# Three seven-product K pairs at the start of the input projection's middle chunk pairs, in a two-layer hybrid trunk

## The chip, the cores and the metric

The kernel runs on one core of a Trainium2 chip, in one launch. The metric is device time in microseconds (us) of that core, as the median of several executions. The engines are named as the profile names them: PE is TensorE (PEld its weight loads), DVE is VectorE, ACT is ScalarE, POOL is GpSimd, SP is SyncE, whose queue carries the weights in. Tiles have 128 partitions.

## What is computed

Two layers over 256 tokens of width 2048, all in float32. Each layer has one combined input projection to 6144 columns, two attentions of eight heads, one output projection, and a gated feed-forward network (FFN):

```python
for l in range(DEPTH):
    h = rms_norm(x, pre_mix_norm[l])
    proj = h @ w_in[l]            # q, k, v of the stick-breaking heads, q, k, v of the differential heads
    m = concat(stick_breaking(proj), differential(proj)) @ w_o[l]
    x = x + rms_norm(m, post_mix_norm[l])
    h = rms_norm(x, pre_ffn_norm[l])
    f = (silu(h @ w_gate[l]) * (h @ w_up[l])) @ w_down[l]
    x = x + rms_norm(f, post_ffn_norm[l])
```

## The kernel before

**Products.** A float32 product is made of three matmuls on rounded operands: hi x hi, hi x lo and lo x hi, where hi is the operand rounded by ACT and lo the rest, taken by DVE (`product`, L1216 to L1221). "A product" below is such a triple of 128x128 by 128x512.

**Tiling.** Weights come in column chunks of 512 and in K pairs: 256 rows of the 2048, so eight K pairs, 0 to 7. One chunk of one K pair is one transfer of 512 KB on SP's queue (L253). The input projection takes its 12 chunks two by two: `PAIRS` lists six chunk pairs, n = 0 to 5. A chunk pair has four accumulators in PSUM, for two halves of the tokens (t = 0, 1) and two chunks: x11, x12 (t = 0), x21, x22 (t = 1). All pairs from n = 1 on use the same four banks.

**Eight or seven products.** A K pair of a chunk pair is a 2 x 2 by 2 x 2 block product. In the ordinary form it takes eight products, 24 matmuls (`eight_in`, L998). In the seven-product form (Strassen's scheme as Winograd arranged it) it takes seven, 21 matmuls, called p1, p6, p7, q5, c11, c12 and c21. They need sums of token blocks, made once per layer (`pair_forms`, L1008, `token_sums`, L1223), and sums of the weight blocks, made each time in place: `mixed_weights` (L276 to L318) takes both chunks of the K pair. The first, a, is rounded like any other (hi L330, lo L340). For the second, b, DVE adds one half (L308), ACT rounds and DVE takes the rest (hi L302, lo L304), DVE makes two more sums (L313, L314), and both are split again into Th and Tl (L302, L304), one of 512 columns and one of 1024. Th and Tl have one buffer each in this stage; hi and lo have six each, which is three K pairs.

**Where sevens were.** The middle pairs, n = 1 to 4, run their K pairs in the order 0, 1, 4, 2, 5, 3, 6, 7 (`IN_ORDER`), with K pairs 4 and 5 as sevens: `seven_products` puts p1, p6, p7 and q5 into four further banks, and `shared_part` (L1257 to L1264) combines these with one copy on ACT and four operations on DVE. When the pair is finished, `settle` adds the result to each accumulator (four additions on DVE, L1039). The last pair, n = 5, works differently: it starts with its two sevens, all in the four accumulators (`sevens_alone`, L1142). There ACT copies an accumulator aside at the moment when it holds exactly the shared part (`kept_part`, L1172), DVE subtracts these copies (L1187 to L1189), and `added_alone` (L1191) settles three accumulators. An ordinary K pair goes between the sevens' last products (`between`). The output projection starts in the same way, with K pairs 4 and 5 of chunks 0 and 1.

**Order.** Each engine works through its own list in program order. The attention of earlier chunk pairs is interleaved with the projection's matmuls. It is paced by a clock that counts TensorE's steps, and `burst` marks the times in which no attention may claim the banks that a seven needs. Weights are asked for through a plan made beforehand (`weight_order`). An ordinary chunk lands in the tag "raw" with four buffers, and the chunks of a seven in another room (`late_room`, tiles named GU). The output projection runs over K pairs in the order `KP_O` (L34). K pair k needs heads 2k and 2k+1 normalised (L715), transposed on TensorE (L729) and scaled into a `mix` tile.

## Time and profile before

| | us |
|---|---|
| median of three runs | 2179.39 |
| the three runs | 2178.74, 2184.57, 2179.39 |
| the profiled execution | 2180.22 |
| its span | 2178.5 |
| granted TensorE clock | 0.999 |
| middle pairs n = 2, 3, 4 of layer 0 | about 45 us each |

The profiled execution lies 0.83 us above the median. In rows of groups the columns are: line, engine, operation, output<-inputs, shapes, count, then busy time and mean ns of one, then idle time of the engine just before and what ended it. In rows of waits they are the time waited in all, how often, and the longest. In rows of a timeline they are start and duration. A row of transfers gives the count, the size and the median time from issue to landing.

### The profile page before, as it was taken

The numbers are of one execution on the slowest core, as the hardware profiler recorded it, in microseconds if no ns is written. First come the engines' busy times: TensorE is split into PE (matmuls) and PEld (weight loads), VectorE is DVE, ScalarE is ACT, GpSimd is POOL, SyncE is SP. The second block draws the span as 40 slices with busy tenths as digits, with TensorE's granted clock in tenths as the row PEclk, the third lists the DMA queues.
The fourth block names the chain that finished last, engine by engine and source line by source line (L and its number), as shares of the span: only waits on it lengthen the run. The fifth ranks groups of instructions, "written<-read, shape, count | busy, mean of one in ns | idle before, by whom it ended". The sixth has DMA issues, their size and how long they took to land.

```text
span 2178.5 us, 28781 instructions
## 1 busy us (share of the span) xinstructions
PE 2161.9 (99%) x9932; PEld 1778.3 (82%) x9932; DVE 1960.4 (90%) x2705; ACT 1414.4 (65%) x2113; POOL 246.5 (11%) x239
## 2 busy tenths in 40 slices
PE   9999999999999999999999999999999999999998
PEld 7888888888888888888878888888888888888886
DVE  7888977899999999999878888778999999999997
ACT  7666775765766666666665667757566666576664
POOL 2100000021221220000010000000212212200000
PEclk9999999999999999999999999999999999999999
DMA  8545446497887877767465564455978877767683
GB/s 324 194 165 200 161 171 199 156 307 230 248 260 225 232 234 233 224 228 253 146 242 174 179 206 155 171 179 184 294 232 253 257 224 237 232 218 241 203 269 99
DMA packets 140275, 470.44 MB, mean 216 GB/s; under 512 B 15952, under 2 KB 16976, under 8 KB 139616
## 3 DMA queue, kind: packets, MB, share of 16 engines
q1 hardware_dynamic: 121952, 436.03, 57.9%
q0 software_dynamic: 17600, 32.02, 8.9%
q8 instruction: 78, 1.28, 0.2%
q14 instruction: 69, 0.57, 0.1%
q10 hardware_dynamic: 576, 0.54, 0.1%
HBM read 460.14 MB, written 8.39 MB: 215 GB/s over the span
## 4 chain that ended last, share of the span: by engine, by line
PE 90%; DVE 5%; ACT 2%; DMA 2%; issue 2%; DVEq 0%; SPq 0%; ACTq 0%
PE c L1351 20%; PE in L1219 7%; PE in L1221 7%; PE in L1220 7%; PE dn L1582 4%; PE dn L1585 4%; PE dn L1583 4%; PE p L1220 3%; PE c L1219 2%; PE c L1220 2%; PE p L1221 2%; PE c L1221 2%; PE p L1219 2%; PE o L629 2%; PE o L631 2%; PE o L630 2%
## 5 line engine op out<-in xcount | busy, mean ns | idle before, releaser
L340 DVE TENSOR_TENSOR lo<-raw,hi 128x1024 fp32r<-128x1024 f32 x448 | 544.0, 1233 | 58.5 <-ACT hi L330 57.4
L330 ACT ACTIVATE hi<-raw 128x1024 fp32r<-128x1024 f32 x470 | 480.1, 1054 | 73.6 <-DMA raw<-in_weights_in_turn_dram 33.2
L1351 PE MATMUL c<-hi,xF 128*128 128x512 f32 x1344 | 364.4, 392 | 0.7 <-DVE xF L539 0.5
L1351 PEld LDWEIGHTS c<-hi,xF 128*128 128x128 f32 x1344 | 249.7, 188 | 53.3 <-ACT act L1469 1.9
L270 POOL DMA_DIRECT2D T<-in_weights_in_turn_dram x122 | 107.6, 882 | 1367.5 <-PE c L1351 541.0
L1351 PE MATMUL c<-lo,xF 128*128 128x512 f32 x672 | 207.4, 390 | 0.0
L302 ACT ACTIVATE Th<-T 128x512 fp32r<-128x512 f32 x122 | 77.2, 633 | 199.4 <-DVE T L313 198.4
L302 ACT ACTIVATE Th<-G 128x1024 fp32r<-128x1024 f32 x122 | 129.0, 1058 | 80.0 <-DVE G L314 78.6
L1582 PE MATMUL dn<-hi,jh 128*128 128x512 f32 x416 | 162.0, 389 | 0.0
L1583 PE MATMUL dn<-lo,jh 128*128 128x512 f32 x416 | 161.8, 389 | 0.0
L304 DVE TENSOR_TENSOR Tl<-G,Th 128x1024 fp32r<-128x1024 f32 x122 | 148.9, 1221 | 11.6 <-ACT Th L302 11.6
L304 DVE TENSOR_TENSOR lo<-T,hi 128x1024 fp32r<-128x1024 f32 x122 | 152.9, 1253 | 0.1
L330 ACT ACTIVATE hi<-G 128x1024 fp32r<-128x1024 f32 x122 | 128.9, 1056 | 36.5 <-DMA G<-in_weights_in_turn_dram 22.1
L314 DVE TENSOR_TENSOR G<-G,T 128x1024 f32<-128x1024 f32 x122 | 148.7, 1219 | 2.6 <-DVE T L313 0.9
L1351 PEld LDWEIGHTS c<-lo,xF 128*128 128x128 f32 x672 | 126.0, 188 | 26.4
L340 DVE TENSOR_TENSOR lo<-G,hi 128x1024 fp32r<-128x1024 f32 x104 | 126.8, 1219 | 10.1 <-ACT hi L330 9.9
L302 ACT ACTIVATE hi<-T 128x1024 fp32r<-128x1024 f32 x122 | 128.0, 1050 | 11.4 <-PE c L1221 8.3
L1585 PE MATMUL dn<-hi,jl 128*128 128x512 f32 x416 | 128.1, 389 | 0.0
L1219 PE MATMUL in<-hi,xT 128*128 128x512 f32 x316 | 125.9, 400 | 1.6 <-DVE xT L929 1.6
L1219 PE MATMUL in<-hi,xI 128*128 128x512 f32 x316 | 126.1, 400 | 0.0
L1220 PE MATMUL in<-lo,xI 128*128 128x512 f32 x316 | 123.5, 391 | 0.3 <-DVE lo L340 0.3
L1221 PE MATMUL in<-hi,xI 128*128 128x512 f32 x316 | 123.2, 391 | 0.0
(522 smaller groups left out, 5028.8 us busy)
## 6 DMA issues: line engine op xcount, KB each, us to landing
raw<-in_weights_in_turn_dram SPq DMA_DIRECT2D x482, 512.0 KB, 4.9
T<-in_weights_in_turn_dram SPq DMA_DIRECT2D x122, 512.0 KB, 5.3
G<-in_weights_in_turn_dram SPq DMA_DIRECT2D x122, 512.0 KB, 5.4
T<-in_weights_in_turn_dram POOLq DMA_DIRECT2D x122, 256.0 KB, 5.6
GU<-in_weights_in_turn_dram SPq DMA_DIRECT2D x48, 512.0 KB, 6.4
V<-in_weights_in_turn_dram SPq DMA_DIRECT2D x8, 512.0 KB, 5.3
away_ffn<-x SPq DMA_DIRECT2D x8, 512.0 KB, 7.2
xd<-away_ffn SPq DMA_DIRECT2D x8, 512.0 KB, 9.2
```

The lines of the kernel that those rows point to most:

```text
L302: nc.scalar.activation(h, w, AF.Copy)
L304: newest_rest[i] = nc.vector.tensor_tensor(out=l, in0=w, in1=h.bitcast(F32), op=ALU.subtract)
L314: nc.vector.tensor_tensor(out=g, in0=g, in1=t2.unsqueeze(1).to_broadcast([P, 2, CW]), op=ALU.add)
L330: nc.scalar.activation(hi, raw, AF.Copy)
L340: rest = nc.vector.tensor_tensor(out=lo, in0=raw, in1=hi.bitcast(F32), op=ALU.subtract)
L1219: nc.tensor.matmul(a, sh, hi, start=first, stop=False, skip_group_check=open_sums[0])
L1220: nc.tensor.matmul(a, sh, lo, start=False, stop=False, skip_group_check=open_sums[0])
L1221: return nc.tensor.matmul(a, sl, hi, start=False, stop=last, skip_group_check=open_sums[0])
L1351: nc.tensor.matmul(a, stat[part], w[j][:, kk, :], start=first and kk + n == 0, stop=last and kk == 1 and n == 2)
L1582: nc.tensor.matmul(accs[c, t], sh, hi[:, kk, :], start=first, stop=False, skip_group_check=open_sums[0])
L1583: nc.tensor.matmul(accs[c, t], sh, lo[:, kk, :], start=False, stop=False, skip_group_check=open_sums[0])
L1585: nc.tensor.matmul(accs[c, t], sl, hi[:, kk, :], start=False, stop=last, skip_group_check=open_sums[0])
```

## The change

The middle pairs now begin with three sevens, K pairs 4, 5 and 6, which share the four accumulators as those of the last pair did. `sevens_alone` takes two or three K pairs. With three, the product c21 of all of them has a bank of its own ("c21_in", `lone`), ACT keeps copies of all four accumulators, and DVE makes four operations (three subtractions, and one that reads the lone bank); `added_alone` then settles three accumulators. The ordinary K pair 0 stands in `between`. The rest follows in the order 1, 2, 3, 7. `seven_in` is gone. The weights of K pair 6 land in the "raw" ring of four buffers, its token sums in a tile of tag "v". In `KP_O`, K pairs 1 and 2 trade places. The last pair keeps its two sevens, and the FFN stays as it was.

```diff
-KP_O = (4, 5, 6, 7, 0, 1, 2, 3)
+KP_O = (4, 5, 6, 7, 0, 2, 1, 3)
...
-IN_SEVEN = (4, 5)
-IN_ORDER = (0, 1, 4, 2, 5, 3, 6, 7)
-IN_LAST = (4, 5, 0, 1, 2, 3, 6, 7)
-IN_NOW = ((), IN_SEVEN, IN_SEVEN, IN_SEVEN, IN_SEVEN, IN_SEVEN)
+IN_SEVEN = (4, 5, 6)
+IN_NOW = ((), IN_SEVEN, IN_SEVEN, IN_SEVEN, IN_SEVEN, IN_SEVEN[:2])
...
 def in_order(n):
 
-    if n == 0:
-        return tuple(range(KT // 2))
-    return IN_LAST if n == len(PAIRS) - 1 else IN_ORDER
+    return IN_NOW[n] + tuple(kp for kp in range(KT // 2) if kp not in IN_NOW[n])
...
                 if kp in IN_NOW[n]:
                     plain.add(lay["in"][cb, kp])
-        aside[lay["in"][PAIRS[-1][1], IN_LAST[1]]] = "v"
+                if kp in IN_NOW[n][2:]:
+                    in_ring.add(lay["in"][cb, kp])
+        aside[lay["in"][PAIRS[-1][1], IN_SEVEN[1]]] = "v"
         order_o = [(c, kp) for kp in KP_O for c in (0, 1)]
         order_o += [(c, kp) for kp in LATE_O for c in (2, 3)] + [(c, kp) for c in (2, 3) for kp in LAST_O]
...
-            elif i in plain or i + 1 in plain:
+            elif {i, i + 1} & (plain - in_ring):
                 raw = late_room([P, 2, CW], f"GU{i}")
             else:
                 raw = wpool.tile([P, 2, CW], F32, tag="raw", bufs=4, name=f"raw{i}")
-            mixing = bool({i, i + 1} & (own | plain))
+            mixing = bool({i, i + 1} & (own | plain - in_ring))
             with not_ahead(i) if mixing else nullcontext():
...
         def sums_of(kp):
-            forms[kp] = pair_forms(pool, pool.sums, len(IN_SEVEN), xT, kp, f"in{l}")
+            if kp == IN_SEVEN[2]:
+                forms[kp] = pair_forms(pool, pool, 2, xT, kp, f"in{l}", tags=("v",))
+            else:
+                forms[kp] = pair_forms(pool, pool.sums, 2, xT, kp, f"in{l}")
...
-                        if alone:
-                            if t + col:
-                                src = added_alone(src, w, t, col, w[(0, 0, 2, 3)[2 * t + col]])
-                        elif w is not None:
-                            src = w[:, 2 * t + col, :]
-                            nc.vector.tensor_tensor(out=src, in0=banks[2 * t + col], in1=src, op=ALU.add)
+                        if mine and t + col:
+                            src = added_alone(src, w, t, col, w[0 if t == 0 else 2 + col], len(mine) == 3)
                         st = heads.setdefault((kind // 3, g), {"w": {}, "pT": {}, "scored": 0})
...
-                extra = None
-                burst[0] = clock[0] + 4 * kps.index(mine[0]) if mine and not alone else None
-                if alone:
+                if mine:
                     open_sums[0] = True
-                    w = pool.tile([P, 4, CW], F32, tag="gpost", bufs=1, name=f"w{l}_{n}")
-                    at = [plan[l]["in"][c, kp] for kp in kps[:2] for c in cc]
+                    if not ending:
+                        burst[0] = clock[0]
+                        assert math.inf not in taken
+                    room = pool.tile([P, 4, CW], F32, tag="gpost", bufs=1, name=f"w{l}_{n}")
+                    w = [room[:, i, :] for i in range(4)]
+                    at = [plan[l]["in"][c, kp] for kp in mine for c in cc]
+                    ordinary = kps[len(mine)]
 
                     def between(t):
-                        eight_in(banks, xT, l, cc, kps[2], (t,), False, False, 2)
-
-                    w = [w[:, i, :] for i in range(4)]
-                    sevens_alone(banks, forms, xT, kps[:2], at, w, between)
-                    kps = kps[3:]
+                        eight_in(banks, xT, l, cc, ordinary, (t,), False, False, 2)
+
+                    sevens_alone(banks, forms, xT, mine, at, w, between, f"c21_in{l}_{n}")
+                    kps = kps[len(mine) + 1 :]
                     ahead = list(KP_O[:2])
+                    if not ending:
+                        burst[:] = (clock[0] + 4 * len(kps) if n + 2 < len(PAIRS) else None), clock[0] + SETTLE
...
-                    if kp in mine and not alone:
-                        if extra is None:
-                            assert math.inf not in taken
-                            extra = four_banks(True, [f"{q}_in{l}_{n}" for q in ("p1", "p6", "p7", "q5")])
-                        seven_in(banks, extra, forms[kp], xT, l, cc, kp, kp == mine[0], kp == mine[-1])
-                        if kp == mine[-1]:
-                            burst[:] = None, clock[0] + SETTLE
-                            w = pool.tile([P, 4, CW], F32, tag="gpost", bufs=1, name=f"w{l}_{n}")
-                            with tc.high_priority(offset=URGENT):
-                                shared_part(extra, [w[:, i, :] for i in range(4)])
-                            if n + 2 < len(PAIRS):
-                                burst[0] = clock[0] + 4 * (len(kps) - 1 - j) + 4 * IN_ORDER.index(IN_NOW[n + 1][0])
-                        continue
...
-    def sevens_alone(banks, sums, tiles, kps, at, w, between):
+    def sevens_alone(banks, sums, tiles, kps, at, w, between, nm):
 
         x11, x12, x21, x22 = banks
-        feed(at[0] + 5)
-        jobs = []
-        for n, kp in enumerate(kps):
+        lone = bank(nm) if len(kps) == 3 else x21
+        feed(at[0] + (6 if len(kps) == 3 else 5))
+        def products_of(n):
+            kp = kps[n]
             hi, lo = ready[at[2 * n]]
             m = ready[at[2 * n + 1]]
             a11, a12, a22 = pair_blocks(tiles, kp)
             s1, s2, s3, s4 = sums[kp]
-            first = n == 0
-            jobs.append({
+            first, last = n == 0, lone is not x21 and n == len(kps) - 1
+            return {
                 "p1": (x11, a11, (hi[:, 0, :], lo[:, 0, :]), first, False),
                 "q5": (x12, s1, m["t1"], first, False),
                 "p7": (x21, s3, m["t3"], first, False),
                 "p6": (x22, s2, m["t2"], first, False),
                 "c11": (x11, a12, (hi[:, 1, :], lo[:, 1, :]), False, False),
                 "c12": (x12, s4, m["b22"], False, False),
-                "c21": (x21, a22, m["t4"], False, False),
-            })
-        a, b = jobs
+                "c21": (lone, a22, m["t4"], first and lone is not x21, last),
+            }
 
         def run(*todo):
             for n, job in enumerate(todo):
@@ -1171,34 +1159,49 @@
             with tc.high_priority(offset=URGENT):
                 nc.scalar.copy(w[j], bank)
 
-        run(a["p1"], a["q5"], a["p7"], a["p6"], b["p1"], b["q5"])
-        kept_part(0, x11)
-        kept_part(3, x12)
-        run(a["c11"], b["c11"])
-        feed(at[0] + 6)
-        run(b["p6"])
-        kept_part(1, x22)
-        run(a["c12"], b["c12"], b["p7"])
-        kept_part(2, x21)
-        between(0)
-        run(a["c21"], b["c21"])
-        between(1)
+        a, b, *rest = (products_of(n) for n in range(len(kps)))
         p1, p6, p7, q5 = w
+        if rest:
+            c = rest[0]
+            run(a["p1"], a["q5"], a["p7"], a["p6"], a["c21"])
+            run(b["p1"], b["q5"], c["p1"], c["q5"])
+            kept_part(0, x11)
+            kept_part(3, x12)
+            run(a["c11"], b["c11"], c["c11"])
+            feed(at[0] + 8)
+            run(b["p7"], b["p6"], b["c21"])
+            run(a["c12"], b["c12"], c["c12"])
+            between(0)
+            run(c["p7"], c["p6"], c["c21"])
+            kept_part(2, x21)
+            kept_part(1, x22)
+            between(1)
+        else:
+            run(a["p1"], a["q5"], a["p7"], a["p6"], b["p1"], b["q5"])
+            kept_part(0, x11)
+            kept_part(3, x12)
+            run(a["c11"], b["c11"])
+            feed(at[0] + 6)
+            run(b["p6"])
+            kept_part(1, x22)
+            run(a["c12"], b["c12"], b["p7"])
+            kept_part(2, x21)
+            between(0)
+            run(a["c21"], b["c21"])
+            between(1)
         nc.vector.tensor_tensor(out=p6, in0=p6, in1=p1, op=ALU.subtract)
         nc.vector.tensor_tensor(out=q5, in0=q5, in1=p1, op=ALU.subtract)
         nc.vector.tensor_tensor(out=q5, in0=q5, in1=p7, op=ALU.subtract)
-
-    def added_alone(acc, w, t, col, to):
-
+        if rest:
+            nc.vector.tensor_tensor(out=p7, in0=lone, in1=p6, op=ALU.subtract)
+
+    def added_alone(acc, w, t, col, to, whole):
+
+        own = t and (col or whole)
         nc.vector.tensor_tensor(
-            out=to, in0=acc, in1=w[3 if t and col else 1], op=ALU.subtract if (t, col) == (1, 0) else ALU.add
+            out=to, in0=acc, in1=w[2 + col if own else 1], op=ALU.subtract if (t, col) == (1, 0) and not whole else ALU.add
         )
         return to
-
-    def seven_in(banks, extra, sums, xT, l, cc, kp, first, last):
-        hi, lo = weights(plan[l]["in"][cc[0], kp], LOOKAHEAD)
-        m = weights(plan[l]["in"][cc[1], kp], LOOKAHEAD)
-        seven_products(banks, extra, sums, *pair_blocks(xT, kp), hi, lo, m, first, last)
...
+        elif tags == ("v",):
+            both = spool.tile([P, 2, 4, P], F32R, tag="v", bufs=2, name=f"ss{nm}")
             sh, sl = both[:, 0], both[:, 1]
                "c21": (lone, a22, m["t4"], first and lone is not x21, last),
+            }
...
+        if rest:
+            c = rest[0]
+            run(a["p1"], a["q5"], a["p7"], a["p6"], a["c21"])
+            run(b["p1"], b["q5"], c["p1"], c["q5"])
+            kept_part(0, x11)
+            kept_part(3, x12)
+            run(a["c11"], b["c11"], c["c11"])
+            feed(at[0] + 8)
+            run(b["p7"], b["p6"], b["c21"])
+            run(a["c12"], b["c12"], c["c12"])
+            between(0)
+            run(c["p7"], c["p6"], c["c21"])
+            kept_part(2, x21)
+            kept_part(1, x22)
+            between(1)
...
+        if rest:
+            nc.vector.tensor_tensor(out=p7, in0=lone, in1=p6, op=ALU.subtract)
...
```

The names in the rows below carry a number at the end, which is the tile's own: in lo_1125 and hi_1123, say. First, VectorE in the third chunk pair (n = 2) of layer 0: before, the second of its two sevens and the ordinary K pairs around it.

```order
L304 TENSOR_TENSOR lo_1149<-GU_1146,hi_1148 128x1024
L340 TENSOR_TENSOR lo_1186<-raw_1182,hi_1184 128x1024
L313 TENSOR_TENSOR GU_1146<-GU_1146 128x512
L340 TENSOR_TENSOR lo_1192<-raw_1188,hi_1190 128x1024
L314 TENSOR_TENSOR GU_1140<-GU_1140,GU_1146 128x1024
L304 TENSOR_TENSOR Tl_1151<-GU_1146,Th_1150 128x512
L304 TENSOR_TENSOR Tl_1151<-GU_1140,Th_1150 128x1024
L340 TENSOR_TENSOR lo_1222<-raw_1218,hi_1220 128x1024
L340 TENSOR_TENSOR lo_1228<-raw_1224,hi_1226 128x1024
L340 TENSOR_TENSOR lo_1261<-raw_1257,hi_1259 128x1024
L1261 TENSOR_TENSOR w_2_1251<-p_in_2_1137,w_2_1251 128x512
L340 TENSOR_TENSOR lo_1267<-raw_1263,hi_1265 128x1024
```

And now, the end of its three sevens (tiles 975 and 981 are K pair 5's weights, 1060 and 1062 K pair 6's):

```order
L311 TENSOR_TENSOR GU_981<-GU_981 128x512
L306 TENSOR_TENSOR raw_1062<-raw_1060,raw_1062 128x512
L312 TENSOR_TENSOR GU_975<-GU_975,GU_981 128x1024
L302 TENSOR_TENSOR Tl_986<-GU_981,Th_985 128x512
L302 TENSOR_TENSOR lo_1069<-raw_1062,hi_1068 128x1024
L302 TENSOR_TENSOR Tl_986<-GU_975,Th_985 128x1024
L311 TENSOR_TENSOR raw_1062<-raw_1062 128x512
L338 TENSOR_TENSOR lo_1125<-raw_1119,hi_1123 128x1024
L312 TENSOR_TENSOR raw_1060<-raw_1060,raw_1062 128x1024
L302 TENSOR_TENSOR Tl_1071<-raw_1062,Th_1070 128x512
L338 TENSOR_TENSOR lo_1129<-raw_1121,hi_1127 128x1024
L302 TENSOR_TENSOR Tl_1071<-raw_1060,Th_1070 128x1024
```

Two sevens' sums stand interleaved where one stood among ordinary rests, and only the next K pair's two rests (lo_1125, lo_1129) are between them.

Second, ScalarE in the same pair. Before, one copy of a bank (p_in) stood among the roundings:

```order
L302 ACTIVATE Th_1150<-GU_1146 128x512
L302 ACTIVATE Th_1150<-GU_1140 128x1024
L330 ACTIVATE hi_1220<-raw_1218 128x1024
L330 ACTIVATE hi_1226<-raw_1224 128x1024
L1260 COPY w_2_1251<-p_in_2_1136 128x512
L330 ACTIVATE hi_1259<-raw_1257 128x1024
L330 ACTIVATE hi_1265<-raw_1263 128x1024
```

Now, with w the place of the kept copies and in_9_1 and in_0_1 the accumulators x21 and x22:

```order
L328 ACTIVATE hi_1123<-raw_1119 128x1024
L328 ACTIVATE hi_1127<-raw_1121 128x1024
L1160 COPY w_2_1058<-in_0_0_1055 128x512
L300 ACTIVATE Th_1070<-raw_1062 128x512
L300 ACTIVATE Th_1070<-raw_1060 128x1024
L328 ACTIVATE hi_1151<-raw_1149 128x1024
L328 ACTIVATE hi_1157<-raw_1155 128x1024
L1160 COPY w_2_1058<-in_9_1_1056 128x512
L1160 COPY w_2_1058<-in_0_1_1057 128x512
```

The copies of x21 and x22 come behind the roundings of K pair 1 (raw_1149, raw_1155), that is, of the K pair after the one that stands in `between`.

Third, TensorE in the output projection of layer 0, before:

```order
L630 MATMUL o_1_1_2905<-lo_3098,mix_sb_0_0_1_3105 128x512
L631 MATMUL o_1_1_2905<-hi_3096,mix_sb_0_0_1_3105 128x512
L729 MATMUL oT_ps_sb_0_1_3249<-ident,on_sb_0_1_3199 128x128 x4
L729 MATMUL oT_ps_sb_1_1_3300<-ident,on_sb_1_1_3266 128x128 x2
L629 MATMUL o_0_0_2902<-hi_3100,mix_sb_0_1_0_3247 128x512
L630 MATMUL o_0_0_2902<-lo_3102,mix_sb_0_1_0_3247 128x512
L629 MATMUL o_0_1_2904<-hi_3100,mix_sb_0_1_0_3247 128x512
L630 MATMUL o_0_1_2904<-lo_3102,mix_sb_0_1_0_3247 128x512
```

And now:

```order
L628 MATMUL o_1_0_2934<-lo_3182,mix_sb_1_0_1_3194 128x512
L629 MATMUL o_1_0_2934<-hi_3180,mix_sb_1_0_1_3194 128x512
L627 MATMUL o_1_1_2936<-hi_3180,mix_sb_1_0_1_3194 128x512
L628 MATMUL o_1_1_2936<-lo_3182,mix_sb_1_0_1_3194 128x512
L629 MATMUL o_1_1_2936<-hi_3180,mix_sb_1_0_1_3194 128x512
L727 MATMUL oT_ps_sb_1_1_3343<-ident,on_sb_1_1_3303 128x128 x4
L627 MATMUL o_0_0_2933<-hi_3218,mix_sb_0_1_0_3284 128x512
L628 MATMUL o_0_0_2933<-lo_3220,mix_sb_0_1_0_3284 128x512
L629 MATMUL o_0_0_2933<-hi_3218,mix_sb_0_1_0_3284 128x512
```

The last two transposes of the stick-breaking heads (on_sb_0_1, on_sb_1_1) stood one behind the other; now the 24 matmuls of K pair 2 (mix_sb_1_0) stand between them, the last five of which are shown.

19 lines of the change are left out of this document (10 added, 9 removed).

## The prediction

> **What bounds the kernel now.** I read the page's busy shares and chain first, then busy time by stretch in the input projection, then what TensorE waits for there.
>
> ```profile
> PE 2161.9 (99%) x9932; PEld 1778.3 (82%) x9932; DVE 1960.4 (90%) x2705; ACT 1414.4 (65%) x2113; POOL 246.5 (11%) x239
> ...
> PE 90%; DVE 5%; ACT 2%; DMA 2%; issue 2%; DVEq 0%; SPq 0%; ACTq 0%
> ```
>
> TensorE is busy 99% of the span and carries 90% of the chain. The next fence has stretches (us, then busy time of each engine, then granted clock): three middle chunk pairs of layer 0 one by one, the middle pairs of both layers, and 500 us of the FFN.
>
> ```profile
> core 0: us, PE busy (x) PEld busy (x) DVE busy (x) ACT busy (x) POOL busy (x), PEclk, DMA share, GB/s
> 85.50:130.70 45.20, 44.97 (x220) 36.06 (x220) 38.51 (x69) 27.42 (x59) 4.57 (x8) 1.00 0.59 211
> 130.70:175.60 44.90, 44.90 (x222) 36.89 (x221) 37.67 (x59) 28.92 (x53) 4.28 (x8) 1.00 0.43 146
> 175.60:220.00 44.40, 44.40 (x212) 35.88 (x211) 36.09 (x57) 28.66 (x48) 0.00 (x0) 1.00 0.55 185
> 85.00:243.00 158.00, 157.77 (x777) 127.68 (x776) 132.72 (x228) 98.36 (x196) 8.85 (x16) 1.00 0.48 169
> 1169.00:1327.00 158.00, 157.75 (x776) 127.62 (x775) 132.79 (x228) 98.67 (x197) 8.89 (x16) 1.00 0.47 161
> 400.00:900.00 500.00, 499.07 (x2253) 412.53 (x2252) 481.02 (x596) 328.66 (x411) 92.86 (x71) 1.00 0.78 240
> ...
> PE pT_df L890 <- DVE w L1262: 0.2, 1, 0.2
> ```
>
> In the middle pairs TensorE is full (157.8 of 158) at clock 1.00, and the only wait listed for it between 85 and 290 us is 0.2 us. So a matmul taken away there is worth its full start-to-start time, as long as VectorE keeps up: it is at 132.7/158 = 84%. In the FFN it runs at 481/500 = 96% while TensorE still stays at 499, so a high VectorE share alone does not stall TensorE; a burst might.
>
> **Part 1, the removed products.** Each of the 4 middle pairs of 2 layers turns one more K pair from 24 matmuls into 21: 8 x 3 = 24 matmuls of 128x512 fewer. A row of the chain gives 24 such matmuls:
>
> ```profile
> 576.12 5.44 PE c L1351 x24
> ```
>
> 5.44/24 = 226.7 ns each, so **-5.44 us**.
>
> The Trainium skill, "TensorE: Matmul & The Clock Gate", section "Back-to-back issue gap", says that a sustained stream of loads and matmuls with N = 512 takes about 131 ns each. By it these 24 would be worth an estimated 3.1 us and the whole forecast would be 2.3 us later. The trace disagrees (226.7 ns) and decides.
>
> **Part 2, the output projection.** K pairs 1 and 2 trade places, and the normalised heads that K pair 2 needs come later than those of K pair 1.
>
> ```profile
> PE oT_ps_sb L729 <- DVE on_sb L715: 0.6, 1, 0.6
> PE oT_ps_sb L729 <- DVE on_sb L715: 0.9, 1, 0.9
> ...
> 330.94 0.60 PE L729 MATMUL oT_ps_sb<-ident,on_sb 128*128 128x128 f32 x4
> 332.13 0.41 PE L729 MATMUL oT_ps_sb<-ident,on_sb 128*128 128x128 f32 x2 [0.59 <-DVE on_sb L715]
> 332.61 0.50 PE L629 MATMUL o<-hi,mix_sb 128*128 128x512 f32 x1
> ...
> 331.29 0.69 DVE L715 TENSOR_TENSOR on_sb<-o_sb,ors_sb 128x512 f32<-128x512 f32 x1
> ...
> 1414.56 0.60 PE L729 MATMUL oT_ps_sb<-ident,on_sb 128*128 128x128 f32 x4
> 1416.03 0.41 PE L729 MATMUL oT_ps_sb<-ident,on_sb 128*128 128x128 f32 x2 [0.87 <-DVE on_sb L715]
> ```
>
> The transposes of the last two normalised tiles stand back to back; the second finds its input ready only at 331.29 + 0.69 = 331.98 us. From the first transpose to the next matmul pass 1.67 us (332.61 - 330.94) for six small matmuls and their refill, about 0.7 us when nothing waits (0.60 + 0.41 less the overlap at the ends), so 1.0 us is lost per layer. Now 24 matmuls (5.44 us) of K pair 2 stand between the two, far more than 0.9. **-2.0 us** in all; bounds 0 (the first of the two tiles becomes the late one, since VectorE is busier ahead of it) and -2.0. Nothing in the trace makes the first late, so I take the upper end.
>
> **Part 3, what VectorE gets.** Mean durations of the forms in the middle pairs of layer 0, two back-to-back instructions, and two of the attention's forms:
>
> ```profile
> L340 DVE TENSOR_TENSOR lo<-raw,hi 128x1024 fp32r<-128x1024 f32 x36 | 42.9, 1218 | 8.4 <-ACT hi L330 8.4
> L1039 DVE TENSOR_TENSOR w<-in,w 128x512 f32<-128x512 f32 x13 | 8.6, 683 | 1.3 <-PE in L1221 1.3
> L304 DVE TENSOR_TENSOR lo<-GU,hi 128x1024 fp32r<-128x1024 f32 x7 | 8.6, 1225 | 5.2 <-ACT hi L302 5.1
> L304 DVE TENSOR_TENSOR Tl<-GU,Th 128x1024 fp32r<-128x1024 f32 x7 | 8.5, 1218 | 1.6 <-ACT Th L302 1.6
> L314 DVE TENSOR_TENSOR GU<-GU,GU 128x1024 f32<-128x1024 f32 x7 | 8.5, 1217 | 0.0
> L308 DVE TENSOR_TENSOR GU<-GU,GU 128x512 f32<-128x512 f32 x7 | 5.1, 723 | 0.0
> L849 DVE TENSOR_REDUCE mx_df<-s_df 128x1 f32<-128x256 f32 x16 | 6.6, 412 | 0.0
> L876 DVE SCALAR_TENSOR_TENSOR e_df<-e_df,sm_df 128x256 f32<-128x256 f32 x7 | 3.3, 477 | 0.0
> ...
> 253.51 2.35 DVE L340 TENSOR_TENSOR lo<-raw,hi 128x1024 fp32r<-128x1024 f32 x2
> ```
>
> Neighbours overlap by 2 x 1.22 - 2.35 = 0.09 us, so a 1024-wide operation costs 1.13 and a 512-wide one 0.60. A seven-product K pair adds L308, L313, Tl 512, L314 and Tl 1024: 3 x 0.60 + 2 x 1.13 = 4.1 us. Settling loses one 512-wide operation per pair (8 before, 7 now), -0.6. So +3.5 us per pair of 45 us, and VectorE goes from 84% to about 92%, below the 96% that the FFN shows. The sums of K pair 6's tokens (14 small operations) lie in pair 0. None of this is on the path by its average.
>
> By the burst it may be. Three sevens now follow each other at the start, and the order lists what stands on VectorE from the first rest of K pair 4 to the last Tl of K pair 6: 14 1024-wide operations and 12 to 14 512-wide ones in the six middle starts (n = 2, 3, 4 of both layers), with 3.0 to 5.5 us of small softmax operations among them. That is 26.0, 29.7 and 28.2 us in layer 0, and 27.8, 28.4 and 28.2 in layer 1. The first hi of K pair 4 needs a buffer: six hold three K pairs, so it comes free 2 x 24 + 3 = 51 matmuls before the pair starts, 51 x 0.2267 = 11.6 us, plus attention matmuls, less one rounding:
>
> ```profile
> L330 ACT ACTIVATE hi<-raw 128x1024 fp32r<-128x1024 f32 x39 | 39.5, 1056 | 3.7 <-PE in L1221 3.1 <-ACT hi L302 0.6
> L837 PE MATMUL s_df<-kT,qT 64*128 64x256 f32 x32 | 4.8, 377 | 0.0
> ...
> ACT hi L330 <- PE in L1221: 9.3, 8, 2.9
> ```
>
> (The last row shows ACT waiting for that release today.) At 4.8/32 = 0.15 us per attention matmul the lead is 11.0 to 12.4 us. TensorE reads the last Tl after 67 or 68 matmuls of the new pair and its attention, 16.1 to 18.1 us. So VectorE has 27.2, 29.7, 27.8 and 28.4, 30.2, 27.8 us for the work above: it is late by -1.2, 0.0, +0.4 and -0.6, -1.8, +0.4. It breaks even. Pair 1 of each layer, behind the slack pair 0, needs 21.3 and 19.0 us and has 25 or more: free.
>
> What remains are VectorE's own waits for ScalarE inside that work, and ScalarE's copies of two accumulators, which stand behind two hi roundings of the next ordinary K pair (first a transfer by itself, then the median of all between 85 and 290 us, of raw and of GU tiles):
>
> ```profile
> DVE lo L304 <- ACT hi L302: 5.3, 6, 1.3
> DVE Tl L304 <- ACT Th L302: 1.6, 3, 0.5
> ...
> raw<-in_weights_in_turn_dram SPq DMA_DIRECT2D x1, 512.0 KB, 3.3
> ...
> raw<-in_weights_in_turn_dram SPq DMA_DIRECT2D x48, 512.0 KB, 4.4
> GU<-in_weights_in_turn_dram SPq DMA_DIRECT2D x16, 512.0 KB, 6.0
> ...
> L1172 ACT COPY w<-in 128x512 f32<-128x512 f32 x4 | 2.2, 584 | 0.0
> ```
>
> Waits: 6.9 us over some 8 sevens, 0.9 each. With three sevens interleaved one fills the gaps of another, so I take a third of 3 x 0.9: 0.9 per start (bounds 0 and 2.6). Copies: the second of those roundings waits for a transfer whose ring slot VectorE frees 1.13 + 1.13 us (two wide operations) before it ends the last Tl. The transfer alone lands in 3.3, then 1.06 to round and 0.58 to copy: the copy ends 4.9 us after the slot is free, 2.7 after the last Tl. TensorE, if it runs right behind VectorE, still has 8 matmuls (1.8 us) after reading that Tl: 0.9 late; with 4.4 to land, 2.0 late; and not late at all where VectorE is ahead by that much. I take 0.4, nearer to the end without a wait, since the ledger has VectorE ahead in three starts of six. With the ledger's mean of -0.5, a start costs -0.5 + 0.9 + 0.4 = 0.8, and 6 x 0.8 = **+4.8 us**; bounds 0 and 6 x (-0.5 + 2.6 + 2.0) = 24.6.
>
> The 24 kept copies, 16 Th and 2 sums on ScalarE are 24 x 0.58 + 16 x 0.85 + 1 = 29 us over 8 pairs, 3.6 each; ScalarE has 45 - 28.7 = 16 us idle per pair. Zero, apart from the place in its order priced above. Transfers are the same, in another order: zero.
>
> **Sum:** -5.44 - 2.0 + 4.8 = -2.6 on the profiled 2180.22, giving 2177.6; that run lay 0.83 above the median 2179.39, so **2176.8**.
>
> **Rivals.** (A) The forecast, one small stall per middle start: 2174 to 2181, chance 0.60.
>
> (B) The other side: the accumulator copies gate every start. The mechanism is a loop through four engines: VectorE frees a raw slot late, SyncE's transfer starts late, the hi rounding waits for it, the copies queue behind it, and TensorE waits for the bank. It decides from the point where the landing takes the median 4.4 us rather than 3.3: then each of six starts loses -0.5 + 0.9 + 2.0 = 2.4, and 14.4 - 7.4 = +7.0 gives 2186.4. For it: VectorE's ledger breaks even with nothing to spare, so lateness adds to the landing. Against it: the last pair already starts with two sevens that share accumulators, with VectorE full and TensorE too:
>
> ```profile
> 240.00:257.00 17.00, 17.00 (x95) 14.04 (x94) 16.80 (x28) 16.94 (x37) 0.00 (x0) 1.00 0.17 54
> ```
>
> With the GU row's 6.0 to land, the copy is 3.6 late and the start 4.0: 24 - 7.4 = +16.6, or 2196, its far end. Chance 0.24.
>
> (C) No stall: the third seven fits as the second does. -7.4: 2172.0. The quoted 17.00 of 17.00 speaks for it, the ledger's break-even against. Chance 0.13.
>
> (D) The swap moves the wait to the first transpose instead, -5.44 + 4.8: 2178.8. Chance 0.03, inside A's range.
>
> **How the numbers follow.** A measurement of this kernel tells about 0.3% (6.5 us) from no change: faster is below 2172.9, slower above 2185.9. C falls mostly under the first, about 0.13; B mostly above the second, and with A's edge 0.22; the rest, 0.65, between. Range: from C's end, 2171.5, to 2189, into B. A's own range is 2174 to 2181.
>
> **What would show it.** Right: 24 fewer 128x512 matmuls; no wait of the transposes of on_sb above 0.2 us; VectorE about 92% in the middle pairs; TensorE waits of 0.3 to 1.5 us at the starts of pairs 2 to 4, most on Tl, lo or a kept copy, and almost none at pair 1. Wrong: waits of over 2 us per start, ended by the copies of the accumulators (B); none at all (C); or stalls in pair 0 or the FFN, which I price at nothing.

## The result: slower by 0.7%, and the profile after

| | before | changed |
|---|---|---|
| median, us (6 runs each) | 2180.70 | 2195.62 |
| lowest to highest, us | 2178.74 to 2186.35 | 2193.99 to 2201.80 |
| ratio to before, 95% interval | | 1.007 [1.006, 1.008] |
| span of the profiled execution, us | 2178.5 | 2192.3 |

The forecast was 2176.8, within 2171.5 to 2189.0. The time lies above the range, 15 us above the kernel before.

The changed kernel's page, busy times and chain:

```profile
PE 2171.8 (99%) x9908; PEld 1777.5 (81%) x9908; DVE 1996.3 (91%) x2751; ACT 1443.3 (66%) x2155; POOL 259.8 (12%) x239
...
PE 86%; DVE 7%; DMA 2%; issue 2%; ACT 2%; POOL 1%; SPq 0%; DVEq 0%; ACTq 0%; POOLq 0%
```

TensorE has 24 fewer matmuls and yet 9.9 us more busy time; its part of the chain fell from 90% to 86%. POOL has the same 239 instructions and 13.3 us more busy time (246.5 before): a hint that something slows it down.

TensorE's waits in the changed kernel, over the whole span (those of the input projection from pair 1 on; total, times, longest, in us):

```profile
PE qkT_ps L1065 <- POOL tok L910: 3.5, 2, 3.1
PE in L1223 <- DVE Tl L302: 2.3, 4, 1.0
...
PE in L1222 <- ACT w L1160: 1.1, 2, 0.9
...
PE in L1223 <- DVE lo L302: 0.6, 1, 0.6
...
PE in L1222 <- DVE w L1201: 0.4, 1, 0.4
PE in L1222 <- ACT Th L300: 0.4, 1, 0.4
...
```

The longest is on POOL, an engine to which the prediction gave no term. The others come from every kind of preparation (Tl, lo, Th, kept copies, settling), none of them large: 4.0 us in the starts of pairs 2 to 4 of both layers, and 0.8 in pair 1 of layer 1.

To see where the time went I took the time of each chunk pair's first matmul from the trace. The table gives lengths in us: pair 1 (layer 0 / layer 1), pairs 2 to 4 of both layers together, the last pair, the output projection, and the sum of all this over both layers. Pair 0 and the FFN have the same work in both kernels; their lengths differ by up to 2 us from one execution to another (pair 0 of layer 0 took 43.7 us in one execution and 45.9 in another, without a pattern), so they are left out. Pairs 2 to 4 of layer 0 took 49.5, 48.4 and 49.7 us in the kernel before, not the 45 that stands ahead of the prediction. They start at 95.7, 145.3 and 193.7 us, so the prediction's three stretches from 85.5 us on are not the pairs. Its 84% for VectorE holds all the same: 161.6 of 192.8 us in the four middle pairs.

| kernel | pair 1 | pairs 2-4 | last pair | output proj. | sum |
|---|---|---|---|---|---|
| before | 45.1 / 45.1 | 295.4 | 52.8 / 52.8 | 95.8 / 95.9 | 682.9 |
| changed | 51.2 / 46.3 | 303.3 | 53.5 / 53.5 | 94.7 / 94.7 | 697.2 |
| e1 trade alone | 45.1 / 45.1 | 295.4 | 52.7 / 52.8 | 94.8 / 94.8 | 680.6 |
| e2 late transposes | 50.1 / 47.0 | 303.5 | 53.5 / 53.5 | 94.7 / 94.7 | 697.0 |
| e3 first rotation out | 45.9 / 45.7 | 305.7 | 53.5 / 53.5 | 94.7 / 94.7 | 693.6 |
| e4 two sevens in pair 1 | 46.3 / 45.2 | 301.7 | 55.3 / 55.6 | 95.7 / 95.7 | 695.6 |
| e5 two sevens everywhere | 50.8 / 45.0 | 296.3 | 55.1 / 55.1 | 94.7 / 94.7 | 691.6 |
| e6 lighter third seven | 53.3 / 46.2 | 304.1 | 53.5 / 53.5 | 94.7 / 94.7 | 699.9 |
| e7 all rotations out | 46.1 / 46.1 | 303.7 | 53.5 / 53.5 | 94.7 / 94.7 | 692.3 |
| e8 three sevens spread | 46.0 / 45.1 | 290.2 | 54.4 / 54.4 | 95.7 / 95.7 | 681.5 |
| e9 own room | 51.6 / 51.9 | 300.9 | 53.5 / 53.5 | 94.7 / 94.7 | 700.8 |
| e10 copies first | 51.6 / 46.5 | 302.9 | 54.2 / 53.6 | 94.7 / 94.7 | 698.2 |
| e11 e9 and e10 | 51.4 / 52.3 | 304.9 | 54.6 / 53.5 | 94.7 / 94.7 | 706.1 |
| e12 e9, e10, rotations out | 47.5 / 45.6 | 300.9 | 54.2 / 54.3 | 94.7 / 94.7 | 691.8 |
| e13 two K pairs between | 53.9 / 46.4 | 296.7 | 57.5 / 57.5 | 95.9 / 95.5 | 703.4 |
| e14 e13, rotations out | 46.4 / 46.0 | 294.8 | 57.5 / 57.5 | 95.4 / 96.4 | 693.9 |

The changed kernel's sum is 14.3 us above before. The output projection gave 2.3 (191.7 to 189.4) and the matmuls should have given 5.4, so the chunk pairs lost 14.3 + 2.3 + 5.4 = 22 us. Per pair, with 0.68 us of removed matmuls added back, 8.7 lie in the two pairs 1 (6.8 in layer 0), 12.0 in the six other starts (2.0 each) and 1.4 in the last pairs. Attention moves between the pairs and into the output projection when the order shifts, so the sum is the surest column. Single cells are less sure: pairs 2 to 4 run the same code in the changed kernel, e2 and e3, and took 303.3, 303.5 and 305.7 us. The table has one execution of each kernel.

### The profile page after: what moved, and what is told of

Read it like the earlier page. It is cut to its first block, busy times and chain, and to the rows that moved or that the text cites. A ratio compares the mean times of both kernels' runs of the same rounds, so it can differ in the third digit from the quotient of the medians.

```text
span 2192.3 us, 28780 instructions
## 1 busy us (share of the span) xinstructions
PE 2171.8 (99%) x9908; PEld 1777.5 (81%) x9908; DVE 1996.3 (91%) x2751; ACT 1443.3 (66%) x2155; POOL 259.8 (12%) x239
## 4 chain that ended last, share of the span: by engine, by line
PE 86%; DVE 7%; DMA 2%; issue 2%; ACT 2%; POOL 1%; SPq 0%; DVEq 0%; ACTq 0%; POOLq 0%
PE c L1357 20%; PE in L1223 5%; PE in L1222 5%; PE in L1224 5%; PE dn L1588 4%; PE dn L1591 4%; PE dn L1589 4%; PE p L1223 3%; PE p L1224 3%; PE c L1222 3%; PE c L1223 3%; PE c L1224 3%; PE p L1222 3%; PE o L629 2%; PE o L627 2%
## 5 line engine op out<-in xcount | busy, mean ns | idle before, releaser
L338 DVE TENSOR_TENSOR lo<-raw,hi 128x1024 fp32r<-128x1024 f32 x440 | 537.6, 1237 | 51.6 <-ACT hi L328 50.1
L328 ACT ACTIVATE hi<-raw 128x1024 fp32r<-128x1024 f32 x462 | 475.3, 1055 | 104.6 <-DMA raw<-in_weights_in_turn_dram 70.8
L312 DVE TENSOR_TENSOR G<-G,T 128x1024 f32<-128x1024 f32 x122 | 149.3, 1224 | 1.9
L338 DVE TENSOR_TENSOR lo<-G,hi 128x1024 fp32r<-128x1024 f32 x104 | 127.2, 1224 | 10.0 <-ACT hi L328 10.0
L1222 PE MATMUL in<-hi,xT 128*128 128x512 f32 x300 | 120.5, 405 | 1.0 <-DVE xT L927 0.6
L1222 PE MATMUL in<-hi,xI 128*128 128x512 f32 x300 | 120.0, 402 | 1.0 <-ACT w L1160 0.9
L1223 PE MATMUL in<-lo,xT 128*128 128x512 f32 x300 | 118.2, 396 | 0.0
L1223 PE MATMUL in<-lo,xI 128*128 128x512 f32 x300 | 117.8, 393 | 0.3 <-DVE lo L338 0.3
```

Of the source, the lines that this page charges most:

```text
L312: nc.vector.tensor_tensor(out=g, in0=g, in1=t2.unsqueeze(1).to_broadcast([P, 2, CW]), op=ALU.add)
L328: nc.scalar.activation(hi, raw, AF.Copy)
L338: rest = nc.vector.tensor_tensor(out=lo, in0=raw, in1=hi.bitcast(F32), op=ALU.subtract)
L1222: nc.tensor.matmul(a, sh, hi, start=first, stop=False, skip_group_check=open_sums[0])
L1223: nc.tensor.matmul(a, sh, lo, start=False, stop=False, skip_group_check=open_sums[0])
```

## Pair 1 of layer 0: the port and the clock

Stretches of the changed kernel around the beginning of its pair 1 (51.8 us):

```profile
core 0: us, PE busy (x) PEld busy (x) DVE busy (x) ACT busy (x) POOL busy (x), PEclk, DMA share, GB/s
57.00:60.00 3.00, 0.56 (x2) 0.19 (x1) 2.96 (x3) 1.43 (x3) 2.92 (x4) 1.00 0.00 0
60.00:61.00 1.00, 0.38 (x3) 0.38 (x4) 1.00 (x2) 0.00 (x0) 0.92 (x2) 1.00 0.00 0
61.00:62.00 1.00, 1.00 (x6) 0.72 (x5) 1.00 (x2) 0.59 (x1) 1.00 (x2) 0.76 0.00 0
62.00:63.00 1.00, 1.00 (x5) 0.65 (x3) 0.51 (x1) 0.00 (x0) 0.97 (x2) 0.50 0.00 0
63.00:64.00 1.00, 0.56 (x4) 0.45 (x3) 0.00 (x0) 0.59 (x1) 0.45 (x1) 0.50 0.00 0
64.00:65.00 1.00, 1.00 (x5) 0.70 (x4) 0.00 (x0) 0.00 (x0) 0.00 (x0) 0.54 0.00 0
65.00:66.00 1.00, 0.96 (x6) 0.60 (x5) 0.00 (x0) 0.89 (x2) 0.00 (x0) 1.00 0.00 0
```

TensorE stands still from 57.6 to 60.6 us, while VectorE and POOL are both full. Then its granted clock (the column after POOL) drops to 0.50 and needs until 65 us to come back: 0.24 + 0.50 + 0.50 + 0.46 = 1.7 us more are lost to the slow clock, which is 3.4 us at half speed. The waiting instruction is a transpose of q or k of pair 0, which POOL must have rotated first:

```profile
60.62 0.66 PE L1065 MATMUL qkT_ps<-ident,tok 128*128 128x128 f32 x4 [3.06 <-POOL tok L910]
```

In the kernel before, the first of these transposes came late in pair 1 (which started at 50.6 us) and found its input ready:

```profile
77.81 0.60 PE L1068 MATMUL qkT_ps<-ident,tok 128*128 128x128 f32 x4
```

Counted in the traces, the transposes of pair 0 stood after 120 to 144 matmuls of pair 1 before. Now they stand after 18 to 24 in layer 0, and in layer 1 four after 25 and the others after 117 to 135; there TensorE didn't wait for POOL. POOL's rows at TensorE's wait, in the timeline (start, duration):

```profile
56.72 0.45 POOL L907 TENSOR_TENSOR ra<-tok,rope_sb 128x128 f32<-128x128 f32 x1
57.14 1.31 POOL L908 TENSOR_TENSOR rb<-tok,rope_sb 128x64 f32<-128x64 f32 x1
58.41 1.29 POOL L909 TENSOR_TENSOR rb<-tok,rope_sb 128x64 f32<-128x64 f32 x1
59.78 0.79 POOL L910 TENSOR_TENSOR tok<-ra,rb 128x128 f32<-128x128 f32 x1
```

The same operations in the kernel before, where VectorE did its sums for the first seven only later:

```profile
48.17 0.46 POOL L909 TENSOR_TENSOR ra<-tok,rope_sb 128x128 f32<-128x128 f32 x1 [12.71 <-ACT tok L1050]
48.60 0.32 POOL L910 TENSOR_TENSOR rb<-tok,rope_sb 128x64 f32<-128x64 f32 x1
48.88 0.32 POOL L911 TENSOR_TENSOR rb<-tok,rope_sb 128x64 f32<-128x64 f32 x1
49.27 0.46 POOL L912 TENSOR_TENSOR tok<-ra,rb 128x128 f32<-128x128 f32 x1
```

A 128x64 operation takes 0.32 us alone, and 1.3 when it waits behind a 1024-wide one of VectorE. VectorE pays too. Its forms in the changed kernel, 50 to 65 us (busy time, mean ns):

```profile
L312 DVE TENSOR_TENSOR GU<-GU,GU 128x1024 f32<-128x1024 f32 x2 | 2.7, 1352 | 0.0
L311 DVE TENSOR_TENSOR GU<-GU 128x512 f32<-128x512 f32 x2 | 1.7, 871 | 0.0
L338 DVE TENSOR_TENSOR lo<-GU,hi 128x1024 fp32r<-128x1024 f32 x1 | 1.5, 1479 | 0.0
```

The Trainium skill states this rule in "SBUF — State Buffer", section "Who interferes with whom": an operation of VectorE with both inputs in SBUF contends with one of GpSimd that reads SBUF, and the shared port is an exclusive lock. The rows above agree (1.3 us for 0.32, 1.48 for 1.22). The prediction didn't weigh it.

## The experiments

e3, e6, e7, e10, e12 and e14 were executed once, e9 and e11 twice. An edit can also change the order into which the instructions are put (as in e9), so a difference need not come from the edited lines alone.

**e1, the trade alone.** The kernel before with one line changed:

```diff
-KP_O = (4, 5, 6, 7, 0, 1, 2, 3)
+KP_O = (4, 5, 6, 7, 0, 2, 1, 3)
```

> The kernel before with only the trade of K pairs 1 and 2 in the output projection. If the trade removes the wait of the on_sb transposes and nothing else: no such wait, both output projections shorter by 1.1 us each (as they are in the changed kernel: 95.83 to 94.74 and 95.91 to 94.72), time about 2.2 us below the kernel before, and input projections of unchanged length (289 and 294 us). Rival, the trade itself costs something in the input projection: its stretches get longer by 1 us or more.

2177.86 against 2179.70, ratio 0.9988 [0.9980, 0.9997]. The wait for on_sb is gone and the two output projections are 2.24 us shorter; nothing else moved. This kernel is faster than both.

**e2, the waiting transposes moved back.** Transposes of pair 0 are issued after the sevens of pair 1.

```diff
+                    with tc.issue_after(sevens_done[0].ins) if c in PAIRS[0] else nullcontext():
                         for j in range(4):
                             nc.tensor.transpose(...)
```

> The changed kernel, with the transposes of the first chunk pair's q and k told to come after the seven-product K pairs of the second chunk pair. Port theory (POOL's rotations of the first pair are slowed by VectorE's operations, TensorE waits for them in the second pair of layer 0, and its clock drops after the wait): no wait of TensorE for POOL, granted clock 1.00 throughout that pair, pair 1 of layer 0 at 46 to 47 us instead of 51.2, time about 2190 to 2191. Load theory (VectorE is too late with the sums of three sevens, POOL only happens to be named): the wait moves to a VectorE operation and pair 1 stays above 50 us, time about 2195.

2193.48, ratio 1.0063 [1.0047, 1.0078]; pair 1 of layer 0 at 50.1. The wait for POOL is gone, but I missed by 3 us, and the length is that of the load theory: TensorE now waits in many short pieces, and the clock still drops (0.67 from 60 to 65 us). Its waits from 50 to 300 us, of which lo, the two hi and one copy of 0.7 lie in pair 1:

```profile
PE in L1225 <- ACT w L1161: 1.8, 4, 0.7
PE in L1226 <- DVE lo L338: 0.5, 1, 0.5
PE in L1226 <- DVE Tl L302: 0.5, 1, 0.5
PE in L1225 <- ACT hi L300: 0.5, 1, 0.5
PE in L1225 <- ACT hi L328: 0.4, 1, 0.4
```

So the wait for POOL was one face of the matter: the weights themselves were late too. VectorE's operations in that start are as long as in the changed kernel, up to 1.49 us.

**e3, the first rotation left out.**

```diff
-                        if kind in (3, 4):
+                        if kind in (3, 4) and n:
                             rotate(pool, tok, t, f"{l}_{c}_{t}")
```

> The changed kernel, leaving out the rotation of the first chunk pair's q and k on POOL (the outputs lack it). Port theory: VectorE's 512-wide operations at the start of pair 1 go back from 0.8 to 0.95 us to 0.68, the 1024-wide ones from 1.34 to 1.48 us to 1.22, no wait of TensorE on POOL, pair 1 of layer 0 at 45.5 to 46.5 us and of layer 1 at 44.5 to 45.5 instead of 51.2 and 46.3. Load theory: the operations keep their lengths, and both pairs stay within 1 us of 51.2 and 46.3.

2188.75. Pair 1 of layer 0 at 45.9 (51.2), of layer 1 at 45.7 (46.3), a little above the forecast for it. VectorE's forms from 49 to 64 us:

```profile
L312 DVE TENSOR_TENSOR GU<-GU,GU 128x1024 f32<-128x1024 f32 x2 | 2.4, 1224 | 0.0
...
L311 DVE TENSOR_TENSOR GU<-GU 128x512 f32<-128x512 f32 x2 | 1.4, 688 | 0.0
...
L338 DVE TENSOR_TENSOR lo<-GU,hi 128x1024 fp32r<-128x1024 f32 x1 | 1.2, 1216 | 0.0
```

1352 back to 1224, 871 to 688, 1479 to 1216, and the clock stays at 1.00. The port theory holds for layer 0: rotations beside the sevens' sums cost its pair 1 5.3 us, clock included. That is near the waits for POOL (3.06 and 0.44) and the 1.7 of the clock, 5.2 together. The other starts stay as slow as they were.

**e4, two sevens in pair 1.** `sevens_alone` was written for two or three K pairs with the lone bank, and:

```diff
-IN_NOW = ((), IN_SEVEN, IN_SEVEN, IN_SEVEN, IN_SEVEN, IN_SEVEN[:2])
+IN_NOW = ((), IN_SEVEN[:2], IN_SEVEN, IN_SEVEN, IN_SEVEN, IN_SEVEN[:2])
```

> The changed kernel with two sevens instead of three in pair 1 (the accumulators still shared, 3 matmuls more per layer), three in pairs 2 to 4. If the third seven's sums on VectorE made pair 1 late: pair 1 of layer 0 at 46 to 47 us, time about 2191. If it is the early start of the sevens beside POOL's rotations, whatever their number: pair 1 of layer 0 stays at 49 us or more, time 2193 to 2196.

2194.48, ratio 1.0067 [1.0054, 1.0081]. Pair 1 of layer 0 came down to 46.3, as the first case said, but the time hardly moved: attention went into the last pairs and the output projections (2 and 1 us longer each). TensorE waited 1.2 us for POOL here and its clock stayed at 1.00. By e5, below, this doesn't show that the third seven had made pair 1 late.

**e5, two sevens in all middle pairs.** The same edit for n = 1 to 4, with 24 matmuls more than the changed kernel.

> The changed kernel with two sevens instead of three at the start of all middle pairs (accumulators still shared, 24 matmuls more). If it is the third seven's sums on VectorE that make the starts late: pairs 2 to 4 back within 0.4 us of the kernel before (49.5, 48.4, 49.7), pair 1 of layer 0 at 46.3 as with two sevens above, time about 2179 to 2181. If starting with sevens in shared accumulators is itself the cost: pairs 2 to 4 stay 1 us or more above it, time 2184 to 2188.

2187.39, ratio 1.0032 [1.0020, 1.0043]. The time is that of the second case. Pairs 2 to 4 are nearly back (296.3 against 295.4), but attention went to the last pairs (55.1). And pair 1 of layer 0 stayed at 50.8, with a wait of 3.1 us for POOL and the clock at 0.66 from 60 to 65 us, though its code is that of e4 and its transposes stand after as many matmuls (18, 19 and 28, the rest after 132 and more). POOL ended the rotation that the second group needs at 60.3 us here and at 58.9 in e4: other operations of VectorE lay beside it. Against e1 the sum is 11.0 higher; without the 5.6 of that pair, 0.7 per start.

**e6, less work on VectorE for the third seven.** L311 and L312 are left out for K pair 6, so its outputs lack them.

```diff
+        if i not in in_ring:
             nc.vector.tensor_tensor(out=t2, in0=t2, in1=u[:, 0, :], op=ALU.subtract)
             nc.vector.tensor_tensor(out=g, in0=g, in1=..., op=ALU.add)
```

> The changed kernel, leaving out two of VectorE's sums (L311 and L312) for the third seven of each middle pair, 1.73 us per start. If VectorE's work ahead of the last Tl sets the starts of pairs 2 to 4: these pairs get shorter by 1 us or more each where they were over 1.5 us late (pairs 3 and 4 of layer 0, 2 and 4 of layer 1), time about 2188 to 2190. If waits for ScalarE's copies or for transfers set them: less than 0.5 us each, time 2193 or more.

Time 2195.53 and pairs 2 to 4 at 304.1: no gain from 1.73 us less per start. In layer 0 TensorE's waits for copies grew instead (0.2 to 1.4). By this one execution, VectorE's amount of work does not set these starts by itself.

**e7, all rotations left out.**

```diff
-                        if kind in (3, 4):
+                        if kind in ():
```

> The changed kernel, leaving out all of POOL's rotations (the outputs lack them). Those of chunks 7 and 9 lie in the starts of pairs 2 and 3. If they slow VectorE there as in pair 1: pairs 2 and 3 of both layers shorter than without the first pair's rotation alone (50.71, 51.03, 50.93, 48.95) by 0.7 us or more each. If not: within 0.3 us of these, and pair 4 unchanged in any case (52).

2188.96, as e3. Pairs 2 and 3 at 51.1, 50.2, 50.7 and 48.2 us, against 50.7, 51.0, 50.9 and 49.0 in e3: 1.5 us less together, not 0.7 each. So the rotations cost little outside pair 1. Sum 692.3.

**e8, three sevens, spread.** The kernel before with the trade, K pair 6 as a third seven in the old form (four further banks), and:

```diff
-IN_ORDER = (0, 1, 4, 2, 5, 3, 6, 7)
+IN_ORDER = (0, 1, 4, 2, 5, 6, 3, 7)
```

> The kernel before with the trade in the output projection and with K pair 6 as a third seven, spread out as before (order 0, 1, 4, 2, 5, 6, 3, 7, four extra banks), so the same 24 matmuls fewer as the changed kernel. If bunching at the start is the cost and not the number of sevens: each middle pair 0.5 to 0.7 us shorter than before, time about 2173 to 2175. If VectorE can't carry three sevens per pair at all: pairs 2 to 4 at or above the kernel before, time 2178 or more. The four extra banks are then held for one K pair longer, which may push attention out of the middle pairs: the last pair would get longer.

2176.89 against 2180.32, ratio 0.9984 [0.9975, 0.9994]: faster than the kernel before, with as many matmuls as the changed one. Pairs 2 to 4 took 290.2, by 5.2 less; the last pairs and output projections are longer, as attention was pushed back. The time lies between the two cases. It is 15.7 us below the changed kernel in the table's sum. Its interval overlaps that of e1. Beside the place of the sevens, their form differs from the changed kernel too: banks of their own, and no kept copies.

**e9, a room of its own for K pair 6's weights.**

```diff
                 if kp in IN_NOW[n][2:]:
-                    in_ring.add(lay["in"][cb, kp])
+                    pass
```

Why I tried it: ScalarE's waits for raw transfers between 85 and 290 us, in the kernel before

```profile
ACT hi L330 <- DMA raw<-in_weights_in_turn_dram: 0.2, 1, 0.2
```

and in the changed one:

```profile
ACT hi L328 <- DMA raw<-in_weights_in_turn_dram: 18.6, 16, 2.7
```

> The changed kernel with K pair 6's weights in the room of the other sevens (GU) instead of the raw ring. Ring theory (the third seven holds two of four raw buffers while it is mixed, so the next transfers start late, hi waits for them and the accumulator copies queue behind): ScalarE's waits for raw transfers between 85 and 290 us fall from 18.6 us to under 6, pairs 2 to 4 of both layers together 303.3 to below 299, time 2189 to 2192. Load theory (three sevens are simply more than VectorE and ScalarE can prepare ahead): the sum stays above 302, time 2194 or more.

2197.99, ratio 1.0074 [1.0045, 1.0103]. Those waits fell to 13.0, pairs 2 to 4 to 300.9: neither case. But pair 1 of layer 1 now lost as much as that of layer 0 (51.9, a wait of 4.2 us for POOL, clock 0.58 from 1156 to 1161 us). In layer 1 the transposes of pair 0 now stand after 21 to 46 matmuls and two after 135. If the ring is a part, it is a small one: 2.4 us, as much as pairs 2 to 4 differ between e2, e3 and the changed kernel.

**e10, the last copies ahead of the next roundings.**

```diff
+            with tc.issue_after(last_copy[0].ins) if i in after_copies else nullcontext():
                 nc.scalar.activation(hi, raw, AF.Copy)
```

> The changed kernel with ScalarE's last two copies put ahead of the two roundings of the next K pair. If the copies gate the starts: no wait of TensorE for a copy (L1160) above 0.2 us in the middle pairs, their sum 303.3 to about 300, time 2192 to 2193. If the roundings then come late themselves: TensorE waits for hi or lo of K pair 1 instead and the sum stays within 1 us of 303.

The edit also has the weights of K pair 1 prepared later, after the first half of `between`. 2193.88; pairs 2 to 4 at 302.9. In layer 1 the wait for a copy fell from 0.9 to 0.2, and a wait for Th (1.3) came up. So the sum is that of the second case, but the wait is not the one that it named.

**e11, e9 and e10 together.**

> Both edits together. If ring and copies are the two halves of one loop, the two gains don't add: sum of the middle pairs as with the better of the two, within 1 us. If they are separate costs, the gains add up (297 or less).

2203.44, ratio 1.0099 [1.0070, 1.0128], both pairs 1 above 51 and pairs 2 to 4 at 304.9. The gains don't add, and don't even stay.

**e12, e9 and e10, and no rotations.**

> Both edits, and POOL's rotations left out (the outputs lack them). If port, ring and copies are all of it, layer 0 from the start of pair 1 to the FFN takes 341.4 - 2.7 - 1.1 = 337.6 us plus at most 3, layer 1 the same, time 2174 to 2179. If starting with three sevens costs beyond these, the stretches stay at 343 or more, time 2184 or more.

2188.38; 346.7 us in layer 0 and 345.2 in layer 1 from pair 1 to the FFN. Starting with three sevens costs beyond port, ring and copies.

**e13, two ordinary K pairs in `between`.**

```diff
-                    ordinary = kps[len(mine)]
+                    ordinary = kps[len(mine) : len(mine) + (1 if ending else 2)]
```

> The changed kernel with two ordinary K pairs (0 and 1) in `between` instead of one, so TensorE has 12 matmuls (2.7 us) more to do before the third seven's last products and before it wants the copied banks; same number of matmuls. If the starts are late because the third seven's sums and the copies of the banks come too late: the middle pairs fall from 303.3 to 300 or less and layer 1 from 345.4 to 343 or less; pair 1 of layer 0, where POOL's rotations decide, stays at 50 us or more; time 2189 to 2193. If the lateness lies earlier, in the first two sevens (lo, settling, first copies): less than 1.5 us of gain, time 2194 to 2196.

The edit also makes the last pair finish the transposes that the output projection's sums need. 2199.50, ratio 1.0081 [1.0064, 1.0097]. Pairs 2 to 4 took 296.7, but attention went to the last pairs (57.5); layer 1 took 347.6 from pair 1 to the FFN. Waits for hi came up (0.5 in layer 0, 0.8 in layer 1). No gain.

**e14, the same without rotations.**

> The same without POOL's rotations (the outputs lack them). If both causes are separate: layer 0 from pair 1 to the FFN at 345 or less (347.4 without rotations and with one K pair between), layer 1 at 343 or less, time 2184 or less. If the delay at the starts is one loop that two more K pairs don't loosen: within 1 us of the run without rotations, 2188 to 2190.

2190.24, sum 693.9 against e7's 692.3; 345.8 us in layer 0 and 348.1 in layer 1. No gain here either.

## Why the prediction was wrong

**Right.** The removed matmuls: 24 fewer. The trade: forecast -2.0, measured -2.3 in the changed kernel and -2.24 alone. VectorE's added work: forecast 3.5 us per pair, measured 3.7 in layer 0 (176.4 us in its four middle pairs, before 161.6); its share came to 87% of 203.6 us and not to 92%, since the pairs got longer.

**The step that failed** is "6 x 0.8 = +4.8", with "Pair 1 of each layer [...]: free". The runs measured 12.0 for the six starts and 8.7 for the two pairs 1, and 1.4 in the last pairs: 22 in all.

*Pair 1 wasn't free.* The prediction counted VectorE's operations at their lengths in stages where POOL was nearly idle (8.85 of 158 us), and had no term for POOL, whose queue the sevens' sums were now moved beside. It did not look at where pair 0's transposes would stand either. The runs show 5.1 to 5.3 us of layer 0's 6.8 there (51.2 to 45.9 in e3, 46.1 in e7): slowed operations on both engines, a wait of 3.06 us, and a clock at half speed for 3.4 us. The Trainium skill, "TensorE: Matmul & The Clock Gate", section "What's actually happening", puts the fall to half clock after an idle window of about 3.4 us. Here one wait of 3.06 us was enough (3.1 in e5), and so was e2's close row of waits of 0.4 to 0.7. The 4.2 us in e9 did it too; 1.2 us in e4 did not.

*Each start costs about 2 us, not 0.8.* Without rotations (e7) and against e1's sum less the matmuls (680.6 - 5.4 = 675.2), eight starts lose 17.1 with the last pairs, or 2.1 each. The ledger of VectorE's work was near. In pair 3 of layer 0 its first and last rows are

```profile
141.64 1.22 DVE L338 TENSOR_TENSOR lo<-GU,hi 128x1024 fp32r<-128x1024 f32 x1 [1.40 <-ACT hi L328]
...
171.66 1.23 DVE L302 TENSOR_TENSOR Tl<-raw,Th 128x1024 fp32r<-128x1024 f32 x1
```

31.3 us from end to end, 30.4 of them busy, for the forecast's 29.7. The lead was 11.7 us (the pair starts at 153.3), within its 11.0 to 12.4. What was wrong is what I made of it: one wait at the last Tl, with one correction for the copies. In the trace TensorE waits at several points (lo, settling, Tl of the second seven, Th, copies). The waits listed come to 4.0 us in the six starts, near the forecast's 4.8 and of the kinds that it named. But the pairs lost 12.0, and pair 4 lost 2.7 us in layer 0 with 0.2 listed, and 2.6 in layer 1 with none. By the starts of TensorE's instructions, 2.7 of the 12.0 lie in attention's matmuls (326, before 334) and 9.2 between those of the products, so about 5 us are delays that the list doesn't have (a matmul's record lasts 0.39 us and the next starts 0.23 us after it, so a start that is 0.1 us late leaves no idle time). What causes them isn't shown. Taking 1.73 us from VectorE (e6), putting the copies first (e10) or giving TensorE other work (e13) moved the listed waits without a gain in the sum.

*Rival B*, which had the right side, named such a loop, and its far end of 2196 is near the time. That is luck: it has 24 us in the six starts, which lost 12.0, and nothing in pair 1. Its mechanism isn't shown to be the cause: the late transfers are there (18.6 us against 0.2), yet the waits for copies are 1.1 us in all, and e10 removed most of them in layer 1 without a gain.

**Settled:** three sevens per pair need not cost 2.1 us. Spread out in the older form (e8), eight pairs lose 681.5 - 675.2 = 6.3, or 0.8 each. Two at the start cost 0.7 each (e5), so number and place both count, and together they cost more than the sum of the two. e8 changed place and form at once; which of them saves the time isn't separated. **Open:** which link of the chain of VectorE, ScalarE and transfers would have to be faster for a start with three. More lead, by a seventh hi and lo buffer, wasn't tried.

## What to carry to other kernels

Price work that is moved in time at the lengths it has beside its new neighbours, and list all engines that are busy there, the lightly loaded one too. Here a burst that broke even in a ledger of one engine lost 2.1 us each time, and the same products spread out lost 0.8. Compare the loss with the waits that the profile lists: in pairs 2 to 4 the list held a third of it. And look at where a new order puts the small instructions of the stage before: pair 0's transposes moved from the last third of pair 1 to its beginning, and a wait of 3 us there cost 1.7 us of clock as well.

## What the runs showed of the hardware

In the changed kernel the granted clock fell to 0.50 about 1 us after TensorE took up work again (from 61 us on, above), and cost 1.7 us. In e9 it fell while TensorE still stood (0.67 from 1153 to 1154 us; the wait ended at 1154.25), stayed there twice as long, and cost (1 - 0.73 + 1 - 0.58) x 5 = 3.5 us. So the moment isn't tied to the end of the wait. POOL's 128x64 operation took 0.32 us alone and 1.3 behind VectorE's 1024-wide one, and VectorE's took up to 1.48 us instead of 1.22.
